# Queries and keys of an attention layer projected with features on partitions, instead of being transposed head by head

## The chip, the cores and the metric

The kernel runs on one core of a Trainium2 chip. The metric is the device time of one execution in microseconds. An execution computes a whole two-layer step of a small hybrid model on 128 context tokens and 1024 latent tokens.

## The reference

Only layer 0's attention matters here. From a normalised, modulated input h (1152 tokens x 1024) the reference projects queries, keys and values of two kinds of heads, rotates those of the second kind, and attends:

```python
nq, nk, nv, dq, dk, dv = split_cols(h @ w_in, ATTN_IN_SIZES)      # 512 columns each

def axial_rope(x):                       # differential heads, latent tokens only
    def rot(xh, p):                      # cos, sin of position p times 16 frequencies
        x1, x2 = xh[..., :quarter], xh[..., quarter:]
        return jnp.concatenate([x1 * cos - x2 * sin, x1 * sin + x2 * cos], axis=-1)
    return jnp.concatenate([rot(xf[..., :half], pos // GRID_W), rot(xf[..., half:], pos % GRID_W)], axis=-1)

def diff_attention(q, k, v, lam, lam_init):
    s = jnp.einsum('bqhcd,bkhcd->bhcqk', qb, k) * scale           # c: two maps a head
    p = jax.nn.softmax(s, axis=-1)
    p = p[:, :, 0] - lam * p[:, :, 1]
    o = jnp.einsum('bhqk,bkhe->bqhe', p, v)

def neighbourhood_attention(q, k, v, k_ctx, v_ctx, rpb):          # 8 x 16 window on a 16 x 64 grid, plus context
    s_win = jnp.einsum('brqhd,brikhd->bhrqik', qg, kg) * scale + bias
```

Keys and values of a 128-token cache are appended; context queries see context keys alone. The context's keys and values (not rotated) are outputs too.

## The kernel before

All is 32-bit. For a precise product each factor is split into a high half, rounded to the fast matmul type, and the low rest, and three matmuls are added (`mm3`). The normalised input is kept with features on partitions: eight tiles hH and hL of 128 features x 1152 tokens.

**Projection.** The columns of the heads are taken in eight groups: groups 0 to 3 are the four differential heads, 4 to 7 pairs of neighbourhood heads. A group has 384 columns: 128 of queries, of keys and of values. `attn_in` (L357) loads eight weight tiles wraw, splits each into wh and wl (L74, L75), and `proj_tok` (L332) computes nine tiles of 128 tokens x 384 columns with hH and hL as the stationary operands (L350 to L352). `sink` copies each tile from PSUM to ist (L368) and stores it to a table qkv in HBM (L369). A generator gives one step for the loads and one for each of the nine tiles.

**Preparing a head.** Scores need queries and keys with features on partitions. `prep_k` (L409) loads the head's keys token by token as kraw (L417, L418, L422), `stage` rotates them (L387 and L394 on VectorE, L397 on POOL), splits them (L405 on ScalarE, L406 on VectorE), and TensorE transposes them (L429) into K, copied by ScalarE (L434, L437). Ten tiles of tokens, two transposes each. `prep_q` (L440) does the same for one 128-token tile of queries: load qraw (L504, or L615 and L617), stage, four transposes (L446), one copy to Q (L448).

**Units and order.** A unit is a head and one of its nine query tiles. Its steps are a (queries), scores (L518, L519; L643 to L647 for neighbourhood heads), and weighted sums, which transpose the probabilities (L476) and multiply by the values (L482). `pipe` (L567) runs 36 units in a software pipeline: in each of 36 + 2 rounds seven slots, each followed by `fill`. `hook` prepares a new head's keys and values at its first unit. In the first stage the units are those of the differential heads, and `fill` pulls 0.28 of a step of the projections of groups 1 to 7 (gs) and 0.3 of a step of `ada_vec` a slot: 128x512 blocks aw of the modulation weights come from HBM (L128) and are accumulated on VectorE (L181). In the second stage the units are neighbourhood heads; bias tiles nab (L624), a mask nam (L587) and gathered values vw (L599, POOL's queue) come in, and `fill` pulls 0.34 of a step of the output projection: input rows xr (L699, L702) transposed to x (L705), attention outputs odr turned to mh and ml (`mix_k`), output weights owraw to owh and owl. Each transfer is on the queue of the engine that issues it; nearly all are on SP's.

The code gives instructions in this order, and a planner in the build, which models the engines' times, moves ready instructions ahead of waiting ones when it writes down each engine's final order. On the chip each engine and queue keeps that order.

## Time and profile before

| | us |
|---|---|
| median of 3 runs | 3835.94 (3829.51 to 3837.39) |
| the profiled execution | 3830.74 |
| its span in the trace | 3829.0 |
| TensorE busy | 3645.9 |
| VectorE busy | 2284.7 |
| ScalarE busy | 1399.5 |
| POOL busy | 1103.7 |

PE is TensorE, PEld its weight loads, DVE VectorE, ACT ScalarE, SP the engine that only issues transfers; SPq and ACTq are the queues of engines. A row of the trace names the line, the engine, the operation, the tile written and those read, how many, and times; "idle" is what the engine stood before such instructions, and behind the arrow what ended it. In rows of waits come the total in us, how many, and the longest. A matmul's busy time contains its latency, which overlaps with the next one's.

### The profile page before, as it was taken

How to read it: one execution, taken by the hardware profiler on the slowest of the kernel's cores; microseconds unless marked ns; L12 is line 12 of the kernel's file. 1: busy time of each engine (PE TensorE's matmuls, PEld its weight loads, DVE VectorE, ACT ScalarE, POOL GpSimd, SP SyncE). 2: the span in 40 equal slices, each digit the busy share in tenths (PEclk: the TensorE clock that was granted, in tenths of full speed). 3: DMA queues.
4: the chain of work that ended last, by engine and by line, in shares of the span. 5: the costliest groups of instructions: out<-in, count | busy, mean ns of one | idle time of the engine just before them, and what ended most of it. 6: DMA issues, size and time to landing. Idle time of an engine off the chain costs nothing.

```text
span 3829.0 us, 66995 instructions
## 1 busy us (share of the span) xinstructions
PE 3645.9 (95%) x24885; PEld 3428.2 (90%) x24885; DVE 2284.7 (60%) x5106; ACT 1399.5 (37%) x3361; POOL 1103.7 (29%) x1450
## 2 busy tenths in 40 slices
PE   7999997999999999999999998999998999999998
PEld 4899996999999999999989886877777899999998
DVE  6578874665855667765253655666666774444434
ACT  3444444555433333225232332233322533334222
POOL 2000002112323324333010323566652322333430
PEclk9999998999999999999999998999999999999999
DMA  6433325542133335433333345222223122223321
GB/s 209 124 91 100 115 77 127 140 106 60 58 99 104 101 101 160 153 113 99 96 122 117 120 135 199 64 75 74 77 65 101 55 62 77 73 74 108 114 89 62
DMA packets 425397, 392.14 MB, mean 102 GB/s; under 512 B 68172, under 2 KB 370376, under 8 KB 423536
## 3 DMA queue, kind: packets, MB, share of 16 engines
q1 hardware_dynamic: 406640, 376.29, 32.5%
q10 hardware_dynamic: 13152, 7.27, 0.7%
q0 software_dynamic: 5280, 4.31, 0.6%
q8 instruction: 197, 3.23, 0.4%
q14 instruction: 128, 1.05, 0.1%
HBM read 289.32 MB, written 98.33 MB: 101 GB/s over the span
## 4 chain that ended last, share of the span: by engine, by line
PE 73%; DVE 8%; DMA 7%; issue 4%; POOL 4%; ACT 2%; SPq 0%; DVEq 0%; ACTq 0%; POOLq 0%
PE mm L82 9%; PE mm L84 9%; PE mm L83 9%; PE A L1724 3%; PE A L1725 3%; PE A L1726 3%; PE o L482 2%; PE mm L350 2%; PE mm L352 2%; PE mm L351 2%; PE E L1724 2%; PE E L1725 2%; PE E L1726 2%; DMA aw<-in_w_ada_dram 2%; PE T L476 1%
## 5 line engine op out<-in xcount | busy, mean ns | idle before, releaser
L729 DVE SCALAR_TENSOR_TENSOR x<-mm,mod,x 128x128 f32<-128x128 f32 (+1 forms) x576 | 279.1, 512 | 263.1 <-PE mm L84 262.3
L1636 POOL TENSOR_TENSOR wl<-raw,wh 128x512 fp32r<-128x512 f32 x120 | 175.0, 1459 | 592.8 <-ACT wh L1635 582.6
L1635 ACT CAST wh<-raw 128x512 fp32r<-128x512 f32 x288 | 178.0, 619 | 294.8 <-PE A L1725 100.3
L181 DVE SCALAR_TENSOR_TENSOR aacc<-aw,v,aacc 128x512 f32<-128x512 f32 x280 | 235.4, 875 | 81.7 <-DMA aw<-in_w_ada_dram 81.7
L350 PE MATMUL mm<-wh,hH 128*128 128x384 f32 x576 | 201.1, 349 | 13.0 <-ACT wh L74 5.8
L352 PE MATMUL mm<-wh,hL 128*128 128x384 f32 x576 | 196.2, 342 | 4.6 <-DVE hL L261 4.6
L351 PE MATMUL mm<-wl,hH 128*128 128x384 f32 x576 | 197.7, 343 | 0.5 <-DVE wl L75 0.4
L82 PE MATMUL mm<-hH,wh 128*128 128x384 f32 x528 | 184.9, 351 | 2.6 <-ACT wh L74 2.6
L84 PE MATMUL mm<-hH,wl 128*128 128x384 f32 x528 | 180.9, 345 | 2.2 <-DVE rst L867 1.8
L83 PE MATMUL mm<-hL,wh 128*128 128x384 f32 x528 | 180.4, 342 | 0.0
L1636 DVE TENSOR_TENSOR wl<-raw,wh 128x512 fp32r<-128x512 f32 x168 | 121.6, 724 | 86.3 <-ACT wh L1635 84.8
L397 POOL TENSOR_TENSOR rm<-rm,rm 128x128 f32<-128x128 f32 (+1 forms) x40 | 27.1, 676 | 464.9 <-DVE rm L387 332.2
L75 DVE TENSOR_TENSOR wl<-wraw,wh 128x256 fp32r<-128x256 f32 (+1 forms) x184 | 88.8, 501 | 109.9 <-ACT wh L74 80.6
L1150 PE MATMUL A<-AR,BK 64*128 64x256 f32 x576 | 119.6, 423 | 31.8 <-DVE KK L1154 19.5
L524 ACT ACTIVATE P<-S,mx 128x384 f32<-128x384 f32 (+1 forms) x200 | 112.2, 570 | 86.3 <-DVE mx L522 84.1
L82 PE MATMUL mm<-mh,owh 128*128 128x384 f32 x384 | 139.4, 378 | 3.7 <-ACT mh L74 2.5
L83 PE MATMUL mm<-ml,owh 128*128 128x384 f32 x384 | 133.2, 347 | 0.0
L84 PE MATMUL mm<-mh,owl 128*128 128x384 f32 x384 | 131.8, 343 | 1.3 <-DVE owl L75 1.3
L350 PEld LDWEIGHTS mm<-wh,hH 128*128 128x128 f32 x576 | 110.4, 192 | 17.9 <-ACT ist L368 8.0
L1150 PEld LDWEIGHTS A<-AR,BK 64*128 64x128 f32 x576 | 77.5, 198 | 54.5 <-issue 18.4
L817 PE MATMUL mm<-wh,hH 128*128 128x256 f32 x432 | 124.0, 290 | 0.0
L818 PE MATMUL mm<-wl,hH 128*128 128x256 f32 x432 | 122.4, 285 | 0.0
(540 smaller groups left out, 12459.7 us busy)
## 6 DMA issues: line engine op xcount, KB each, us to landing
raw<-in_w_ffn_in_dram SPq DMA_DIRECT2D x176, 256.0 KB
aw<-in_w_ada_dram SPq DMA_DIRECT2D x160, 256.0 KB
raw<-hdr SPq DMA_DIRECT2D x132, 192.0 KB
hdr<-c SPq DMA_DIRECT2D x160, 144.0 KB
raw<-in_w_ffn_out_dram SPq DMA_DIRECT2D x88, 256.0 KB
F<-stg SPq DMA_DIRECT2D x34, 640.0 KB
stg<-st SPq DMA_DIRECT2D x12, 1536.0 KB
qkv<-ist SPq DMA_DIRECT2D x72, 192.0 KB
```

Of the source, the lines that this page charges most:

```text
L82: mm(out, lhsT=wh, rhs=xh, start=first, stop=False)
L83: mm(out, lhsT=wh, rhs=xl, start=False, stop=False)
L84: mm(out, lhsT=wl, rhs=xh, start=False, stop=last)
L181: nc.vector.scalar_tensor_tensor(acc[:, c, :], w[:, 0, :], s, acc[:, c, :], op0=ALU.mult, op1=ALU.add)
L350: mm(pt[:, :ncol], lhsT=hH[k][:, c], rhs=WH[k], start=k == 0, stop=False)
L351: mm(pt[:, :ncol], lhsT=hH[k][:, c], rhs=WL[k], start=False, stop=False)
L352: mm(pt[:, :ncol], lhsT=hL[k][:, c], rhs=WH[k], start=False, stop=k == KT - 1)
L729: self.nc.vector.scalar_tensor_tensor(x[f][:, c], pt[:, a:b], self.mod[l][jg][:, f, cd : cd + 1], x[f][:, c], op0=ALU.mult, op1=ALU.add)
L1150: mm(pts[h][:, j * 256 : j * 256 + 256], lhsT=BK[hs, j, :], rhs=AR[hs], start=True, stop=True)
L1636: eng.tensor_tensor(wl, w, wh, op=ALU.subtract)
L1724: mm(o, lhsT=wh[:, ks], rhs=xh, start=new and k == 0, stop=False, skip_group_check=True)
L1725: mm(o, lhsT=wh[:, ks], rhs=xl, start=False, stop=False, skip_group_check=True)
```

## The change

The projection computes queries and keys with the weights as the stationary operand, so that they come out with features on partitions, in three token groups of 384; the queries and keys of differential heads are rotated right behind it on those tiles (halves swapped by copies across partitions, one multiplication each with tables of sine and cosine that now have features on partitions, one addition). They are split there, and high and low half are stored to a table qf for each of queries and keys. The order of the features within a differential head is changed in the weights' split so that the swap moves 64 partitions at a time. Values are still needed with tokens on partitions: they are projected in the same way and transposed three at a time (`turn`), and stored to vt. Neighbourhood queries are put in the order of their windows when they are split and stored (`patches`, `store_hl`).

A head is prepared by a generator `heads_steps`: K and three tiles Q of 384 queries are loaded as they are, in transfers of 32 or 64 rows (of differential and neighbourhood heads; the stores have 128); only the cached keys are still staged and transposed. `heads_hook` starts it three units ahead of the head. The stepping of the projections becomes 0.53 of a step a slot, for 19 steps a group. Two of the four mix buffers are given elsewhere: three stay and one is opened for the last group.

```diff
...
-        for T in range(NT):
-            pt = self.t(self.nps, [P, 512], tag="mm")
-            c = slice(T * P, (T + 1) * P)
-            for k in range(KT):
-                mm = nc.tensor.matmul
-                mm(pt[:, :ncol], lhsT=hH[k][:, c], rhs=WH[k], start=k == 0, stop=False)
-                mm(pt[:, :ncol], lhsT=hH[k][:, c], rhs=WL[k], start=False, stop=False)
-                mm(pt[:, :ncol], lhsT=hL[k][:, c], rhs=WH[k], start=False, stop=k == KT - 1)
-            sink(T, pt)
...
+        if g < 4:
+            ok, ov = O[4][0, 0, :, j].rearrange("t c d -> t (c d)"), O[5][0, 0, :, j]
+        else:
+            ok, ov = (o[0, 0, :, 2 * j : 2 * j + 2].rearrange("t c d -> t (c d)") for o in (O[2], O[3]))
+        apart = lambda t: [t.rearrange("p (m r s d) -> p s m r d", r=4, s=2, d=16)[:, s] for s in range(2)] if g < 4 else [t]
+        dense = lambda t: [t.rearrange("p (m s r d) -> p s m r d", r=4, s=2, d=16)[:, s] for s in range(2)] if g < 4 else [t]
+        WH, WL = [], []
+        for k in range(KT):
+            raw = self.t(pool, [P, GW], tag="wraw")
+            src = w[k * P : (k + 1) * P, :].rearrange("p (m c) -> p m c", c=512)[:, blk : blk + 3, j * P : (j + 1) * P]
+            nc.sync.dma_start(raw.rearrange("p (m c) -> p m c", c=P), src)
+            wh = self.t(pool, [P, GW], F32R, tag="wh")
+            wl = self.t(pool, [P, GW], F32R, tag="wl")
+            for a in zip(dense(wh), dense(wl), apart(raw)):
+                self.split(*a)
+            WH.append(wh)
+            WL.append(wl)
+        yield
+        def turn(st, n):
+            pt = self.t(self.nps, [P, 512], tag="T")
+            for i in range(n):
+                nc.tensor.transpose(pt[:, i * P : (i + 1) * P], st[:, i * P : (i + 1) * P], self.ident)
+            o = self.t(pool, [P, GW], tag="ist")[:, : n * P]
+            for a in zip(apart(o), dense(pt[:, : n * P])):
+                nc.scalar.copy(*a)
+            return o
+        later = []
+        for m, scale in ((1, None if g < 4 else -0.125), (0, 0.125 if g < 4 else None), (2, None)):
+            ms = slice(m * P, (m + 1) * P)
+            for tg in range(TG):
+                for step in later:
+                    step()
+                later = []
+                sl = slice(tg * GW, (tg + 1) * GW)
+                pt = self.t(self.nps, [P, 512], tag="mm")
+                for k in range(KT):
+                    self.mm3(pt[:, :GW], WH[k][:, ms], WL[k][:, ms], hH[k][:, sl], hL[k][:, sl], k == 0, k == KT - 1)
+                if m == 2:
+                    st = self.t(pool, [P, GW], tag="ist")
+                    nc.scalar.copy(st, pt[:, :GW])
+                    yield
+                    o = turn(st, 3)
+                    dst = self.vt[g][sl, :]
+                    nc.sync.dma_start(dst.rearrange("(n p) c -> p n c", p=P), o.rearrange("p (n c) -> p n c", c=P))
+                    if tg == 0:
+                        nc.scalar.dma_start(ov, o[:, :P])
+                    yield
+                    continue
+                hl = self.t(pool, [P, 2, GW], F32R, tag="hl")
+                hi, lo = hl[:, 0, :], hl[:, 1, :]
+                x = pt[:, :GW]
+                if g < 4 or m == 1 and tg == 0:
+                    n = GW if g < 4 else P
+                    x = self.t(pool, [P, GW], tag="fx")
+                    nc.scalar.copy(x[:, :n], pt[:, :n])
+                    a = P if tg == 0 else 0
+                    sw = lo.bitcast(F32)
+                    for s in range(2):
+                        nc.scalar.copy(sw[64 * s : 64 * s + 64, a:], pt[64 - 64 * s : 128 - 64 * s, a:GW])
+                    ts = slice(tg * GW + a - P, (tg + 1) * GW - P)
+                    nc.vector.tensor_tensor(sw[:, a:], sw[:, a:], self.sin[:, ts], op=ALU.mult)
+                    nc.vector.tensor_tensor(x[:, a:], x[:, a:], self.cos[:, ts], op=ALU.mult)
+                    nc.vector.tensor_tensor(x[:, a:], x[:, a:], sw[:, a:], op=ALU.add)
+                    yield
+                if m == 1 and tg == 0:
+                    nc.sync.dma_start(ok, turn(x, 1))
+                if g >= 4:
+                    x = pt[:, :GW]
+                for u, v in self.patches(g, m, tg):
+                    nc.scalar.activation(v(hi), u(x), AF.Copy, scale=scale or 1.0)
+                if g >= 4:
+                    yield
+                def rest(g=g, m=m, tg=tg, x=x, hl=hl, scale=scale):
+                    hi, lo = hl[:, 0, :], hl[:, 1, :]
+                    for u, v in self.patches(g, m, tg):
+                        if scale is None:
+                            nc.vector.tensor_tensor(v(lo), u(x), v(hi), op=ALU.subtract)
+                        else:
+                            nc.vector.scalar_tensor_tensor(v(lo), u(x), scale, v(hi), op0=ALU.mult, op1=ALU.subtract)
+                    self.store_hl(g, m, tg, hl)
+                if g < 4:
+                    later.append(rest)
+                    rest()
+                yield
+    def patches(self, g, m, tg):
+        if g < 4 or m == 1:
+            same = lambda t: t
+            return [(same, same)]
+        n0 = P if tg == 0 else 0
+        out = [(lambda t: t[:, :n0],) * 2] if n0 else []
+        u = lambda t: t[:, n0:].rearrange("p (r w c) -> p r w c", w=4, c=16)
+        v = lambda t: t[:, n0:].rearrange("p (w r c) -> p r w c", w=4, c=16)
+        return out + [(u, v)]
+    def store_hl(self, g, m, tg, hl):
+        dst, a, hl = self.qf[g][m], tg * GW, hl.bitcast(F32)
+        if g < 4 or m == 1:
+            nc.sync.dma_start(dap(dst, a, [[TOK, P], [P * TOK, 2], [1, GW]]), hl)
+            return
+        r0, n0 = (0, P) if tg == 0 else (6 * tg - 2, 0)
+        nr = (GW - n0) // 64
+        for i in range(2):
+            if n0:
+                nc.sync.dma_start(dap(dst, i * P * TOK, [[TOK, P], [1, n0]]), hl[:, i, :n0])
+            sw = hl[:, i, n0:].rearrange("p (w r c) -> p w r c", w=4, c=16)
+            for rh in range(2):
+                a, b = max(r0, 8 * rh), min(r0 + nr, 8 * rh + 8)
+                if a < b:
+                    o = dap(dst, i * P * TOK + (1 + 4 * rh) * P + (a - 8 * rh) * 16, [[TOK, P], [P, 4], [1, (b - a) * 16]])
+                    nc.sync.dma_start(o, sw[:, :, a - r0 : b - r0, :].rearrange("p w r c -> p w (r c)"))
+    def heads_steps(self, g, cache, p, ps, head, values=None):
+        K = head["K"] = self.t(p, [P, 2, 10 * P], F32R, tag="K")
+        rows = lambda c: [(0, 32 * c, 32), (32, 64 + 32 * c, 32)] if g < 4 else [(0, 64 * c, 64)]
+        for c in range(2):
+            for i in range(2):
+                for o, r, n in rows(c):
+                    o += 64 * i
+                    nc.sync.dma_start(K[o : o + n, c, :TOK].bitcast(F32), dap(self.qf[g][1], (i * P + r) * TOK, [[TOK, n], [1, TOK]]))
+        raw = self.t(p, [P, P], tag="kraw")
+        nc.sync.dma_start(raw, cache)
+        yield
+        def queries(tg):
+            Q = head["Q", tg] = self.t(p, [P, 2, 2, GW], F32R, tag="Q")
+            for c in range(2):
+                for i in range(2):
+                    for o, r, n in rows(c):
+                        o += 64 * i
+                        src = dap(self.qf[g][0], r * TOK + tg * GW, [[TOK, n], [P * TOK, 2], [1, GW]])
+                        nc.sync.dma_start(Q[o : o + n, c, :, :].bitcast(F32), src)
+        queries(0)
+        yield
+        st = self.t(p, [P, 2, 2, 64], F32R, tag="st")
+        for c in range(2):
+            rv, sv = raw[:, 64 * c : 64 * c + 64], lambda i: st[:, c, i, :]
+            if g < 4:
+                rv = rv.rearrange("p (r s d) -> p s r d", s=2, d=16)
+                sv = lambda i: st[:, c, i, :].rearrange("p (s r d) -> p s r d", s=2, d=16)
+                nc.scalar.copy(sv(0), rv)
+                nc.vector.tensor_tensor(sv(1), rv, sv(0), op=ALU.subtract)
+                self.split(sv(0), sv(1), rv, -0.125)
+        yield
+            nc.tensor.transpose(pt[:, c * P : (c + 1) * P], st[:, c].rearrange("p b c -> p (b c)").bitcast(F32), self.ident)
+        nc.scalar.copy(K[:, :, 9 * P :], pt[:, : 2 * P].rearrange("p (c t) -> p c t", c=2))
+        yield
+        queries(1)
+        yield
+        if values is not None:
+            values()
+        yield
+        queries(2)
+        yield
+    def heads_upto(self, j, k, heads, gen):
+        if j not in heads:
+            heads[j] = {"n": 0}
+            heads[j]["gen"] = gen(j, heads[j])
+        while heads[j]["n"] < k:
+            heads[j]["n"] += 1
+            next(heads[j]["gen"], None)
+    def heads_hook(self, j, T, heads, gen):
+        self.heads_upto(j, 7 if T >= 2 else 6, heads, gen)
+        if T >= 6 and j < 7:
+            self.heads_upto(j + 1, (2, 4, 6)[T - 6], heads, gen)
...
+    def diff_prep(self, j, head, p, ps):
         nc, I = self.nc, self.I
-        src = self.qkv[j]
-        K = self.prep_k(j, I["cache_diff_k"][0, 0, :, j].rearrange("t c d -> t (c d)"), True, p, ps)
-        V = self.t(p, [P, 10, P], tag="V")
-        nc.sync.dma_start(V[:, 0:9, :], src[:, 2 * P :].rearrange("(n p) c -> p n c", p=P))
-        nc.sync.dma_start(V[:, 9, :], I["cache_diff_v"][0, 0, :, j])
-        ob = self.t(p, [P, NT, P], tag="ob")
-        ss = self.t(p, [P, NT], tag="oss", bufs=2)
-        return K, V, ob, ss
+        def values():
+            V = head["V"] = self.t(p, [P, 10, P], tag="V")
+            nc.sync.dma_start(V[:, 0:9, :], self.vt[j].rearrange("(n p) c -> p n c", p=P))
+            nc.sync.dma_start(V[:, 9, :], I["cache_diff_v"][0, 0, :, j])
+        return self.heads_steps(j, I["cache_diff_k"][0, 0, :, j].rearrange("t c d -> t (c d)"), p, ps, head, values)
...
-            raw = self.t(p, [P, 1, P], tag="qraw")
-            nc.sync.dma_start(raw[:, 0, :], self.qkv[j][T * P : (T + 1) * P, 0:P])
-            st["Q"] = self.prep_q(p, ps, raw, None if T == 0 else (self.cos[:, T - 1 : T, :], self.sin[:, T - 1 : T, :]))
+            if T == 0:
+                head[j]["ob"] = self.t(p, [P, NT, P], tag="ob"), self.t(p, [P, NT], tag="oss", bufs=2)
...
-            K, Q = head[j][0], st["Q"]
+            K, Q = head[j]["K"], head[j]["Q", T // 3][:, :, :, T % 3 * P : T % 3 * P + P]
...
+    def na_prep(self, j, head, p, ps):
+        hs = slice(2 * j, 2 * j + 2)
+        return self.heads_steps(4 + j, self.I["cache_na_k"][0, 0, :, hs].rearrange("t c d -> t (c d)"), p, ps, head)
...
-        mh = self.t(p, [P, TOK], F32R, tag="mh", bufs=4)
-        ml = self.t(p, [P, TOK], F32R, tag="ml", bufs=4)
+        mh = self.t(p, [P, TOK], F32R, tag="mh")
+        ml = self.t(p, [P, TOK], F32R, tag="ml")
...
-                self.wpool = _Bufs(wp, {"wraw": 3, "wh": 9, "wl": 9, "ist": 2, "aw": 2})
+                self.wpool = _Bufs(wp, {"wraw": 3, "wh": 9, "wl": 9, "ist": 2, "fx": 2, "hl": 2, "aw": 2})
...
-            return self.attn_in(g, hH, hL, wpool)
+            yield from self.first if g == 0 else self.attn_in(g, hH, hL, wpool)
+            done.add(g)
...
-        GS, AS, OS = 0.28, 0.3, 0.34
+        GS, AS, OS = 0.53, 0.3, 0.34
...
-        bp = _Bufs(both.enter_context(self.pool("kAB")), {"K": 2, "Q": 3, "pT": 2, "qraw": 2, "kraw": 2})
+        bp = _Bufs(both.enter_context(self.pool("kAB")), {"K": 2, "Q": 3, "pT": 2})
...
-            fin(self.first)
+            first = group(0)
+            for _ in range(12):
+                next(first)
+            self.heads_upto(0, 5, head, lambda j, h: self.diff_prep(j, h, dp, ps))
+            fin(first)
             self.nps = ps
             gs = itertools.chain.from_iterable(group(g) for g in range(1, 8))
+            def prep(j, h):
+                while j not in done:
+                    next(gs)
+                return self.diff_prep(j, h, dp, ps) if j < 4 else self.na_prep(j - 4, h, dp, ps)
             def hook(i):
-                j, T = divmod(i, NT)
-                if T == 0 and j < 4:
-                    head[j] = self.diff_prep(j, dp, ps)
+                if i < 4 * NT:
+                    self.heads_hook(*divmod(i, NT), head, prep)
...
-        op = _Bufs(self.oA, {"owraw": 1, "owh": 4, "owl": 4})
-        head = {}
+        op = _Bufs(self.oA, {"owraw": 1, "owh": 4, "owl": 4, "mh": 3, "ml": 3})
...
-                    head[j] = self.na_prep(j, dp, ps)
+                if i < 4 * NT:
+                    self.heads_hook(4 + i // NT, i % NT, head, lambda j, h: self.na_prep(j - 4, h, dp, ps))
...
-                    yield from self.mix_k(k, op, ps, ms)
+                    yield from self.mix_k(k, op if len(ms) < 3 else _Route(op, {"mh": more, "ml": more}, None), ps, ms)
...
+            more = es.enter_context(self.pool("oM"))
```

165 lines of the change are left out of this document (34 added, 131 removed).

## The prediction, made before the change was run

> **What bounds the kernel now.** I read the busy times first, then stretches of time cut at the borders of layer 0's stages, then what TensorE waited for in each, then its order of instructions.
>
> ```profile
> span 3829.0 us, 66995 instructions
> PE 3645.9 (95%) x24885; PEld 3428.2 (90%) x24885; DVE 2284.7 (60%) x5106; ACT 1399.5 (37%) x3361; POOL 1103.7 (29%) x1450
> ...
> core 0: us, PE busy (x) PEld busy (x) DVE busy (x) ACT busy (x) POOL busy (x), PEclk, DMA share, GB/s
> 61.00:130.00 69.00, 59.69 (x325) 57.20 (x325) 38.60 (x77) 20.61 (x44) 10.91 (x11) 0.93 0.43 123
> 130.00:604.00 474.00, 459.91 (x2980) 447.73 (x2979) 354.55 (x886) 223.94 (x722) 23.97 (x37) 0.99 0.32 96
> 604.00:670.00 66.00, 38.12 (x206) 33.70 (x205) 29.45 (x79) 27.37 (x74) 21.60 (x32) 0.74 0.67 159
> 670.00:893.00 223.00, 212.24 (x1602) 206.24 (x1601) 135.71 (x404) 122.81 (x315) 21.51 (x32) 0.98 0.45 116
> ```
>
> The change lies between 61 and 893 us. Four stretches: the projection of group 0 (start), differential attention with the other seven projections filled in (stage A), the crossing, and neighbourhood attention with the output projection filled in (stage B). TensorE is busy for 97% of A and 95% of B, VectorE for 75% and 61%: in A and B time is TensorE time. The crossing is different: 28 of its 66 us TensorE stands.
>
> ```profile
> PE mm L350 <- ACT wh L74: 5.2, 3, 3.4
> PE mm L350 <- ACT ist L368: 3.2, 6, 1.3
> ...
> PE T L476 <- DVE P L541: 9.2, 2, 7.7
> PE T L429 <- DVE st L406: 8.9, 4, 3.8
> PE S L643 <- DVE mx L649: 3.7, 4, 2.8
> PE T L705 <- DMA xr<-in_x_prompt_dram: 3.1, 1, 3.1
> ...
> PE T L446 <- ACT K L437: 2.3, 1, 2.3
> ```
>
> The first two rows are A's longest waits (us in total, times, longest): small. The others are from 600 to 900 us. Two of them, 8.9 and 2.3 us, are TensorE waiting for the staging of keys and queries that the change removes; the longest (9.2) is not.
>
> What a transpose costs cannot be had from its mean duration, since matmuls overlap. The order of TensorE's instructions (start, duration) gives it:
>
> ```profile
> 593.19 0.60 PE L476 MATMUL T<-ident,P 128*128 128x128 f32 x4
> 593.55 0.42 PE L350 MATMUL mm<-wh,hH 128*128 128x384 f32 x1
> 593.81 0.34 PE L351 MATMUL mm<-wl,hH 128*128 128x384 f32 x1
> 593.99 0.34 PE L352 MATMUL mm<-wh,hL 128*128 128x384 f32 x1
> ...
> L446 PE MATMUL T<-ident,st x288: 271/273/477, 127.9 to 870.9; 128*128 128x128 f32 x144
> L429 PE MATMUL T<-ident,st x160: 270/273/476, 108.5 to 832.4; 128*128 128x128 f32 x160
> ```
>
> Four transposes hold the array from 593.19 to 593.55, 0.36 us or 0.09 each. The wide matmul behind them takes 0.26 to the next start, where one among its like takes 0.18: each block costs 0.08 more. A block of four is 0.44 us, 0.11 a transpose. The 273 ns of the rows is latency. The rows also count what there is: 288 query transposes (4 for each of 72 units) and 160 of keys (20 a head).
>
> **The projection itself: no change.** 216 matmuls of 128x384 a group before; after, 3 column blocks x 3 token groups x 8 x 3 = 216 of the same width.
>
> **Transposes, the main term.** Removed: 288 + 160. Added for each of 8 groups: three blocks of three for the values, one for the context keys; for each head one block of two for the cached keys. With 0.09 a transpose and 0.08 a block:
> - Stage A and start: removed 36 blocks of four, 15.8 us, and 80 key transposes at 0.11, 8.8 us. Added 8 x (3 x 0.35 + 0.17) = 9.8 us and five cached blocks at 0.26, 1.3 us (head 4 is prepared in A now). Net 13.5 us less.
> - Stage B: removed 15.8 + 8.8, of which head 4's keys and first query, 2.6 us, stand in the crossing; added 3 x 0.26 = 0.8. Net 21 us less.
> TensorE runs without gaps in both, so I take A at 13 and B at 21. Bounds: if its work were wholly the limit, 35 together; if other engines took over at once, 0.
>
> **Key staging at a head's first unit.** It was emitted at the first unit; now loads start three units ahead. The 8.9 us waits on L429 are 5.3 in the crossing and 3.6 at 693 to 700 us. I take the 3.6 in B.
>
> **The crossing.**
>
> ```profile
> 607.03 1.04 ACT L74 CAST owh<-owraw 128x1024 fp32r<-128x1024 f32 x1 [3.87 <-DMA owraw<-in_w_out_attn_dram]
> 619.25 1.97 PE L476 MATMUL T<-ident,P 128*128 128x128 f32 x8 [7.66 <-DVE P L541]
> 635.51 1.97 PE L429 MATMUL T<-ident,st 128*128 128x128 f32 x8 [3.81 <-DVE st L406]
> 637.25 0.52 DVE L587 CAST nam<-sb 80x512 fp32r<-80x512 f32 x1 [1.72 <-DMA sb<-in_k_namask_dram]
> 655.96 0.30 PE L705 MATMUL T<-ident,xr 128*128 128x128 f32 x1 [3.10 <-DMA xr<-in_x_prompt_dram]
> ```
>
> Until 624 us ACT's in-order queue stands behind output weights that arrive late, and VectorE behind ACT; that stays. The keys of head 4 go out of 624 to 637, with 5.3 + 2.3 us of waits. But the mask tile is copied only at 637.25 and input rows still arrive late at 655.96: these are late next. Removing nothing that ends a wait gives 0; all 28 us idle would be the other bound. I take 6, nearest to the 7.6 of waits, less something for what stays. Other engines there: ten query loads and four key loads leave the crowded transfers too.
>
> **VectorE and ScalarE: covered, in A.**
>
> ```profile
> L387 DVE TENSOR_TENSOR rm<-qraw,cos x32: 281/292/295, 121.6 to 572.4; 128x128 f32<-128x128 f32 x32
> L387 DVE TENSOR_TENSOR rm<-kraw,cos x8: 682/692/693, 104.2 to 487.6; 128x512 f32<-128x512 f32 x8
> L406 DVE SCALAR_TENSOR_TENSOR st<-qraw,st x40: 272/282/295, 101.7 to 868.5; 128x128 fp32r<-128x128 f32 x40
> L448 DVE CAST Q<-T 128x512 fp32r<-128x512 f32 x35 | 24.1, 688 | 9.2 <-PE T L446 8.6
> L75 DVE TENSOR_TENSOR wl<-wraw,wh 128x384 fp32r<-128x384 f32 x47 | 26.5, 578 | 8.9 <-ACT wh L74 8.6
> L368 ACT COPY ist<-mm 128x384 f32<-128x384 f32 x60 | 28.9, 481 | 56.6 <-PE mm L352 52.6 <-issue 2.8 <-ACT wh L74 0.7
> ```
>
> VectorE, a differential head: before, keys 2 x 3 x 0.69 + 0.4, queries 8 x 2 x 0.29 + 9 x (0.28 + 0.69), weight splits 8 x 0.58: 22.6 us. After, rotation 6 x 3 x 0.56 (between 0.29 and 0.69), the low halves 6 x 0.56, and sixteen half-width splits at 0.36: 19.2 us. A neighbourhood group now takes its six low halves in A, some 3.9 us at 0.6. For all: -14 + 16 = +2 us on 354.55. ScalarE: a differential group gets 6 x 4 copies at 0.48 where it had nine copies, two dozen small casts and six key copies, about +3; a neighbourhood group +2; +20 us on 223.94 of 474. Both are hidden behind TensorE; if that cover went, the 20 us of ScalarE would count in part. POOL loses its additions, which nobody on the path waited for long: 0. In B, VectorE and ScalarE each lose about 40 us, also 0 by themselves.
>
> **Queues.** Transfers issued by SP between 61 and 893: stores 72 before; after, 10 a differential group (6 halves, 3 values, 1 keys) and 17 a neighbourhood group (3 + 10 + 3 + 1): 108. Head loads 15 a head before; 35 a differential head after (8 keys, 1 cache, 24 queries, 2 values), 19 a neighbourhood head: 120 becomes 216. ACT's queue loses eight output stores. So SP issues 132 more, at 0.32 to 0.59 us:
>
> ```profile
> L369 SPq DMA_DIRECT2D qkv<-ist x72: 319/322/503, 87.2 to 600.1; - x72
> L617 SPq DMA_DIRECT2D qraw<-qkv x32: 574/592/1761, 572.8 to 860.1; - x32
> SPq L369 <- ACT ist L368: 174.5, 53, 8.1
> SPq L128 <- DVE aacc L181: 39.7, 19, 9.7
> DVE aacc L181 <- DMA aw<-in_w_ada_dram: 7.6, 13, 1.0
> ```
>
> At 0.45 that is 59 us, spread over 830. SP already waits 174.5 us for stores' data, so it has room. Behind it are the modulation weights (aw), for which VectorE waits, in order, with everything queued behind: 7.6 us in A so far. A differential head's loads come in bursts of 17, 10 and 8 issues; the longest holds SP some 7.5 us, more than the 6.3 us between two aw loads (0.3 of a step a slot, seven slots in 474 / 36 = 13.2 us). Lower bound 0; upper, one such burst fully exposed at each of eight heads, 60 us. VectorE stands idle a quarter of A, so I take 4 us lost. POOL's queue keeps its 64 value gathers. Bytes: A moves 474 us x 96 GB/s = 45 MB; keys and queries are now stored as two halves and the queries read for both halves of the partitions, 1.2 MB more a group and 2.4 MB more a head, 20 MB in all. The share of 0.32 becomes about 0.46: hidden.
>
> **Weights at a group's start.** Steps are half as long (0.53 a slot for 19 steps, instead of 0.28 for 10), so from the last matmuls of a group to the first of the next there are 3 / 0.53 = 5.7 slots instead of 2 / 0.28 = 7.1: 2.7 us less to reload eight weight tiles, whose splits took 105.08 to 116.06 us at the first group. Bounds 0 and 7 x 2.7 = 19; the wait so far is 5.2, so I take 3 lost.
>
> **Start and end.** Keys come first and need all token groups early, but TensorE already waits for the low half of the input there, and head 0's staging runs behind group 1's matmuls: 0 (from +8 to -10). The last output group has three mix buffers and one opened late: 1 lost.
>
> **Sum:** -13 - 21 - 3.6 - 6 + 4 + 3 + 1 = -36 us. The profiled execution took 3830.74, so 3795; the median shown, 3835.94, is 5 above it, so 3800 for a median.
>
> **Rivals.**
> 1. *The crossing closes* (more gain). With queries ready, neighbourhood scores need only mask and bias; of the 28 us idle perhaps 18 go instead of 6, and bursts cost nothing (4): 3784 as median. Against: the mask at 637 and the late rows at 656.
>
> ```profile
> 630.00:640.00 10.00, 4.67 (x20) 3.78 (x21) 4.95 (x16) 2.74 (x6) 4.75 (x8) 0.50 0.97 183
> 640.00:650.00 10.00, 7.82 (x34) 7.28 (x34) 3.74 (x15) 4.64 (x16) 4.26 (x7) 0.50 0.84 204
> ```
>
> The granted clock is 0.50 in these 20 us, behind the gaps, and the 12.5 us of work in them would take 6 at full clock: a shorter gap saves up to 6 more, 3778. The Trainium skill, "TensorE: Matmul & The Clock Gate", "What's actually happening", states this as a rule: half clock after an idle window of about 3.4 us, full clock again after a busy one. The two rows agree with it; no run here shows yet whether the gap falls short enough.
> 2. *Another engine takes over* (no change): with TensorE lighter, VectorE's chains (28.9 us it waited on ScalarE's exponentials in A) set the pace; A, B and the crossing give only 10, and 8 are lost: about 3834. For it: 75% with bursts; against: TensorE's small waits.
> 3. *SP becomes the bound* (slower): stores wait for VectorE's low halves, loads for stores, aw stands behind both, VectorE behind aw. At the full 60 us instead of 4: -40 + 60 = +20, 3856. It decides once more than two thirds of the bursts are exposed. Against: 132 issues are 59 us of an idle queue. The Trainium skill, "DMA: Bandwidth & Descriptors", "Anatomy of one DMA", says that a wait sits on the issuing sequencer, not on the DMA engines; the 174.5 us row agrees.
> 4. *The change doesn't do what it says*: transposes were taken into gaps and their removal opens gaps: as 2.
>
> **How the numbers follow.** Forecast (gain of 10 to 50) 0.60; crossing closes, 0.18; no change, 0.09; slower, 0.13. 0.2% is about 7.7 us, what a measurement can tell from no change here: faster 0.78, same 0.09, slower 0.13. The forecast's own range is 3786 to 3826. For 8 in 10 I reach down to 3768 (crossing and the clock, with spread) and up to 3834, the no-change case; beyond are the slow case and a tail of the first.
>
> **What would show it.** Transposes by keys and queries fall from 448 to 96 with the values' included; A is 8 to 16 us shorter, B 18 to 26; no wait for staging at the first unit of a head. Wrong if VectorE's wait for aw grows past 20 us, if the first matmul of a group waits for wh more than 15 us in all, or if TensorE's busy share in A falls below 94%.

## The result: slower by 1.15%

The changed kernel takes 3879.47 us (median of 4, 3874.71 to 3882.32) against 3836.24 (median of 4, 3829.51 to 3837.39): ratio 1.0115, 95% interval 1.0098 to 1.0133. The profiled execution took 3877.96, 47 us more than the one before. The page's span and busy times of the kernel after:

```profile
span 3876.2 us, 66185 instructions
...
PE 3656.6 (94%) x24533; PEld 3436.9 (89%) x24533; DVE 2240.5 (58%) x5030; ACT 1392.4 (36%) x3329; POOL 1068.0 (28%) x1410
```

TensorE issues 352 instructions less and is busy longer. The stretches of layer 0 after, cut where the stages now lie (columns as before: TensorE, its weight loads, VectorE, ScalarE, POOL, granted clock, DMA share, GB/s):

```profile
61.00:130.00 69.00, 54.55 (x278) 50.02 (x276) 47.69 (x111) 28.15 (x76) 9.10 (x8) 0.88 0.50 147
130.00:618.00 488.00, 461.29 (x2882) 445.33 (x2881) 338.55 (x846) 235.90 (x747) 0.00 (x0) 0.97 0.46 131
618.00:687.00 69.00, 44.10 (x214) 40.25 (x213) 23.87 (x72) 23.18 (x62) 21.10 (x32) 0.65 0.81 177
687.00:911.00 224.00, 200.35 (x1381) 195.46 (x1381) 105.02 (x332) 98.82 (x230) 21.92 (x33) 0.90 0.62 144
```

In A the share (0.46) and TensorE's part (94.5%) are as forecast, but A is 14 us longer (488 against 474) where 13 less were forecast. In B TensorE's 212 us busy at clock 0.98 became 200 at 0.90, the transfers' share went from 0.45 to 0.62, and the stretch is as long as before (224 against 223). Below, the stages are cut at the first and last starts of their scores instead, which is the same cut in every kernel; by it 1 us is lost up to the first neighbourhood score (645.4 and 646.6 us) and 15 in B (234.8 and 249.4).

**Where the 47 us lie.** The first FFN matmul starts at 1012.3 us before and 1034.3 after: 22 us are lost in attention. The recurrent scan's first matmul starts at 2341.6 and 2366.2, its last starts at 2899.6 and 2948.7: 24.5 us more are lost in the scan, whose code the diff does not touch. The stretches between and behind agree within 3 us. In the profiles the scan's stretch reads, before, after, and in the kernel with one added memset (e5, below):

```profile
2341.00:2900.00 559.00, 516.55 (x4040) 426.50 (x4040) 373.33 (x869) 172.26 (x409) 321.98 (x735) 0.95 0.30 86
```
```profile
2366.00:2949.00 583.00, 536.51 (x4038) 446.84 (x4040) 365.21 (x869) 173.92 (x407) 322.88 (x735) 0.91 0.29 82
```
```profile
2362.00:2920.00 558.00, 518.51 (x4036) 427.13 (x4036) 368.86 (x869) 172.21 (x408) 321.60 (x735) 0.95 0.30 86
```

The same number of instructions, but in another written order: 706 of TensorE's 1160 scan instructions (runs of one kind counted once) stand elsewhere than before; in e5, 10 do. In the changed kernel's order single waits are longer and the clock is lower (after first, then e5):

```profile
PE A L1217 <- DVE KK L1221: 23.6, 13, 3.7
```
```profile
PE A L1217 <- DVE KK L1221: 19.6, 17, 1.5
```

The order is not all of it. In e16 (below) TensorE's instructions of the scan stand exactly as in e5, and yet its profiled execution, the slowest of twelve, spent 575 us there, at a lower clock:

```profile
2350.00:2925.00 575.00, 542.11 (x4038) 449.40 (x4036) 374.56 (x867) 171.93 (x407) 319.91 (x733) 0.91 0.28 83
```

So single profiles of one order differ by 17 us, and by 24 in e6 and e9 (experiment 3), as much as the loss. That 20 us hang on the later order is read from medians: 3879 with the changed kernel's order and 3855 in e5, and no execution of either lies in the other's range. By what the order acts is not shown.

**The transposes did go.** Those of queries, keys and values are now 72 + 8 + 16 = 96, where 448 stood:

```profile
L361 PE MATMUL T<-ident,ist x72: 270/273/422, 111.5 to 620.7; 128*128 128x128 f32 x72
...
L361 PE MATMUL T<-ident,fx x8: 271/300/477, 92.6 to 559.2; 128*128 128x128 f32 x8
```
```profile
L499 PE MATMUL T<-ident,st x16: 270/273/282, 111.1 to 838.5; 128*128 128x128 f32 x16
```

To see what that was worth I took the time from each TensorE record's start to the next one's start, and put what lies behind an instruction's end aside as a gap. For the two kernels with a barrier behind attention (e1, e2: nearly the same later order), 3427 and 3287 records between 50 and 640 us, 1866 and 1659 from 640 us to the first norm:

| records, us | start, A, crossing: before | after | B and the last group: before | after |
|---|---|---|---|---|
| all transposes | 550, 60.1 | 403, 45.5 | 598, 67.8 | 393, 49.4 |
| matmuls of the projections | 1728, 316.9 | 1728, 320.9 | 408, 75.9 | 408, 78.3 |
| scores of 128x384 | 384, 75.0 | 384, 78.4 | 128, 28.1 | 128, 27.6 |
| bias selection, short scores, weighted sums | | | 732, 88.8 | 730, 100.3 |
| gaps | 45.3 | 49.7 | 16.7 | 42.8 |

Transposes give 14.6 and 18.4 us, close to the 13.5 and 21 forecast. In B the gaps take back 26 and the wider spacing of the other matmuls 13.

What the gaps from 640 us to the first norm wait for after the change (e2, TensorE's longest, then VectorE's waits for transfers):

```profile
PE S L710 <- DVE mx L716: 18.0, 5, 10.2
PE T L549 <- ACT pT L551: 8.2, 3, 7.4
PE o L555 <- DVE ost L735: 6.8, 7, 2.0
PE T L772 <- DMA xr<-in_x_prompt_dram: 3.6, 1, 3.6
PE T L828 <- DMA xr<-odr: 3.4, 2, 2.5
```
```profile
DVE sb L716 <- DMA nab<-rpbd: 27.1, 8, 9.5
DVE ost L735 <- DMA odr<-ost: 8.1, 2, 5.2
```

Most of it is transfers, or VectorE that waits for transfers: the bias tiles nab first (27.1 us; 4.6 in e1), then stored outputs and input rows. The busy tenths of the 16 DMA engines from 640 to 900 us, 6.5 us a digit, before and after, show the difference:

```profile
DMA  8996566762459953222224986752200034352003
...
DMA packets 42954, 31.88 MB, mean 123 GB/s; under 512 B 5298, under 2 KB 41758, under 8 KB 42928
```
```profile
DMA  6788989677987999887716915898965351222251
...
DMA packets 40715, 40.29 MB, mean 155 GB/s; under 512 B 6510, under 2 KB 38102, under 8 KB 40694
```

Before, full stretches alternate with stretches of 2 and 3; after, they are full for most of 200 us. The megabytes grew by a quarter, the number of packets did not. An average of 0.45 was no free half. Where a transfer is late (here stored outputs), TensorE stands and then runs slowly:

```profile
810.00:820.00 10.00, 6.67 (x28) 6.48 (x28) 2.32 (x11) 2.82 (x7) 5.18 (x9) 0.50 0.90 163
820.00:830.00 10.00, 9.99 (x44) 9.90 (x44) 3.07 (x10) 2.94 (x6) 2.66 (x4) 0.50 1.01 169
850.00:860.00 10.00, 10.00 (x74) 10.00 (x73) 5.54 (x15) 2.67 (x8) 0.00 (x0) 1.00 0.23 62
```

The second and third are stretches without gaps: at half clock TensorE got through 44 instructions, at full clock through 74. The clock rule that the prediction cites from the Trainium skill ("TensorE: Matmul & The Clock Gate", "What's actually happening") is half clock after an idle window of about 3.4 us and full clock after a busy one. The rows agree with half clock behind gaps, but not with the lengths: the longest of the gaps in the first row is 2.4 us, and the second row is 10 us without a gap at half clock.

### The profile page after: what moved, and what is told of

The parts are those of the page before. It is cut to its first block, busy times and chain, and to the rows that moved or that the text cites. A ratio compares the mean times of both kernels' runs of the same rounds, so it can differ in the third digit from the quotient of the medians.

```text
span 3876.2 us, 66185 instructions
## 1 busy us (share of the span) xinstructions
PE 3656.6 (94%) x24533; PEld 3436.9 (89%) x24533; DVE 2240.5 (58%) x5030; ACT 1392.4 (36%) x3329; POOL 1068.0 (28%) x1410
## 4 chain that ended last, share of the span: by engine, by line
PE 62%; DMA 7%; DVE 5%; POOL 4%; issue 2%; ACT 1%; SPq 0%; ACTq 0%; DVEq 0%; POOLq 0%
PE mm L82 9%; PE mm L84 9%; PE mm L83 8%; PE A L1791 3%; PE A L1792 3%; PE A L1793 3%; PE E L1791 2%; PE E L1792 2%; PE E L1793 2%; DMA F<-stg 2%; POOL MB L1268 1%; PE o L555 1%; PE A L1217 1%; PE mm L884 1%; POOL tf L1267 1%
## 5 line engine op out<-in xcount | busy, mean ns | idle before, releaser
L796 DVE SCALAR_TENSOR_TENSOR x<-mm,mod,x 128x128 f32<-128x128 f32 (+1 forms) x576 | 278.7, 512 | 257.5 <-PE mm L84 256.8
L82 PE MATMUL mm<-hH,wh 128*128 128x384 f32 x1104 | 389.0, 353 | 23.2 <-ACT wh L74 11.1
L83 PE MATMUL mm<-hL,wh 128*128 128x384 f32 x1104 | 380.0, 344 | 9.4 <-DVE hL L261 9.4
L84 PE MATMUL mm<-hH,wl 128*128 128x384 f32 x1104 | 380.4, 346 | 3.0 <-DVE rst L934 2.4
L82 PEld LDWEIGHTS mm<-hH,wh 128*128 128x128 f32 x1104 | 212.4, 193 | 38.9 <-ACT wh L74 13.4
L670 POOL DMA_DIRECT2D vw<-vt x64 | 43.0, 677 | 696.8 <-DVE nab L653 569.0
L83 PEld LDWEIGHTS mm<-hL,wh 128*128 128x128 f32 x1104 | 213.1, 193 | 12.5 <-DVE hL L261 9.7
L84 PEld LDWEIGHTS mm<-hH,wl 128*128 128x128 f32 x1104 | 212.5, 193 | 8.1 <-issue 2.9
L75 DVE TENSOR_TENSOR wl<-wraw,wh 128x256 fp32r<-128x256 f32 (+2 forms) x216 | 91.3, 447 | 112.3 <-ACT wh L74 83.1
L886 PE MATMUL mm<-wh,hL 128*128 128x256 f32 x432 | 122.0, 283 | 0.0
```

The costliest lines, as they stand in the source:

```text
L82: mm(out, lhsT=wh, rhs=xh, start=first, stop=False)
L83: mm(out, lhsT=wh, rhs=xl, start=False, stop=False)
L84: mm(out, lhsT=wl, rhs=xh, start=False, stop=last)
L796: self.nc.vector.scalar_tensor_tensor(x[f][:, c], pt[:, a:b], self.mod[l][jg][:, f, cd : cd + 1], x[f][:, c], op0=ALU.mult, op1=ALU.add)
```

## The experiments

Single executions of one kernel spread over 20 to 30 us here, and A's last score over some 8, so medians are compared as differences to the kernel before of the same call, whose medians were 3831 to 3836. Most kernels carry a barrier or an unread memset behind attention, only to give the scan the order it had before, or nearly.

**1. Splitting attention from what follows.** e1 and e2 are before and after with

```diff
             xp, x, np_, hp, hH, hL = self.attn(hp, hH, hL, wes)
+            tc.strict_bb_all_engine_barrier()
```

> The kernel before, with one barrier of all engines behind layer 0's attention, so that the planner starts the rest from the same point in every kernel that has it. Both theories: the barrier costs the overlap of the last norm with the first feed-forward matmuls, 0 to 8 us over the kernel before; the scan (2342 to 2900 us in the trace of before, 559 us from the first to the end of its matmuls on L1150 and L1296) stays within 5 us of that.

> The changed kernel with the same barrier. In it the planner gives the scan nearly the order of the kernel before (29 of 1156 of its TensorE instructions stand elsewhere, against 706 in the changed kernel). Theory: of the 43 us lost about 22 are in the attention and 24 in the scan, lost to the planner's other order alone; then this kernel is 18 to 28 us above the one before with the barrier, and its scan takes 559 us within 6. Rival: the scan is slower for another reason (clock, place of its data in memory); then it is 40 to 48 us above, and the scan takes about 583 us.

e1: 3829.45, 5 below the kernel before (ratio 0.999, 0.9977 to 1.0004). e2: 3860.44, 26 above (1.006, 1.0043 to 1.0076). So attention alone loses, and the rest of the loss goes with the later order. e5 shows the latter without a barrier, by a memset that nothing reads:

```diff
+            with self.pool('pad') as pp:
+                nc.vector.memset(self.t(pp, [P, 64], tag='pad'), 0.0)
```

> The changed kernel, without a barrier, with one more instruction: VectorE clears a 128x64 tile that nobody reads, between layer 0's attention and its feed-forward. With it the planner writes the scan in the order of the kernel before but for 10 of 1160 TensorE instructions. Theory, the scan's loss of some 24 us is the planner's order alone: 3853 to 3865, and a scan of 558 us within 5 (first L1150-matmul to last L1296-matmul of the kernel before). Rival, another reason: 3875 to 3884, and a scan of 583.

3854.97, 23 above (1.006, 1.0037 to 1.0083): 20 us of the 43 come back, and the scan takes 558 us again in its profile.

**2. Is it the queue or the shape of the transfers?** e3 issues the loads of K and Q from ScalarE's queue; e7 changes how many rows a transfer has (loads of keys 128, of queries 64, stores 32 or 64).

```diff
-                    nc.sync.dma_start(K[o : o + n, c, :TOK]...
+                    nc.scalar.dma_start(K[o : o + n, c, :TOK]...
```

> As the changed kernel with the barrier, but keys and queries of the heads are loaded from ScalarE's queue instead of SP's; the order behind the barrier is that of the kernel before with the barrier. Theory A, SP's order: small transfers (bias, input rows, modulation weights) stand behind the heads' loads on SP; then 8 to 20 us less than the changed kernel with the barrier. Theory B, the 16 transfer engines themselves are full in these bursts, whichever queue issues: within 5 us of it. If ScalarE's time for issuing (some 150 of 0.4 us) counts: up to 15 us more.

> The changed kernel with the barrier; keys (and the differential heads' queries) are stored so that a head's keys come back in two transfers of 128 rows instead of eight of 32 or four of 64, and the differential queries in four of 64 instead of eight of 32; the stores are of 32 or 64 rows instead. The same bytes, with the clear instruction. Theory shape: 10 to 25 us less than the changed kernel with the barrier. Theory bytes: within 6 of it. If short stores hurt as much as short loads: up to 8 more.

e3: 3873.17, 39 above (1.0091, 1.0062 to 1.0121). e7: 3863.83, 32 above (1.0083, 1.0059 to 1.0108). Neither is better than e2. In e7's profile B takes 250.1 us, as in e2 (250.3), so rows don't matter there. In e3's it takes 257.0: another queue gains nothing, though ScalarE's time for issuing could hide a gain of SP's, which these runs don't separate.

**3. Are bytes hidden?** First from the changed kernel: e4 loads the keys twice, e6 leaves the low query half away for one half of the partitions.

```diff
+                    for _ in range(2):
                         nc.sync.dma_start(K[o : o + n, c, :TOK]...
```
```diff
-                nc.tensor.matmul(S[:, :ch], lhsT=Q[:, c, 1, :], rhs=kk, start=False, stop=True)
+                nc.tensor.matmul(S[:, :ch], lhsT=Q[:64, c, 1, :], rhs=kk[:64], start=False, stop=True)
```

> As the changed kernel with the barrier, but every head's keys are loaded twice (1.2 MB more a head, the same result); behind the barrier the order is that of the kernel before with the barrier. If the heads' loads are what costs the attention its time: 8 to 25 us more than the changed kernel with the barrier, most of it in the neighbourhood stage, where the transfers' share is 0.9 already. If the loss lies in PSUM, weights or the order of the projections: within 4 us.

> The changed kernel with the barrier; the low half of a query is loaded for one half of the partitions only, and its product runs over 64 rows (it leaves out the product of the two low halves). A quarter of the queries' bytes fewer: 0.59 MB a head, 4.7 MB in all, with as many transfers. The same clear instruction keeps the planner's order of the rest. Theory bytes: doubling the keys cost 22 us for 9.4 MB, so 9 to 14 us less than the changed kernel with the barrier (3860.4). Theory shape (transfers of 32 and 64 rows are what is slow, whatever their bytes): 0 to 6 less. Theory PSUM and weights: within 3.

e4: 3882.38, 48 above (1.012, 1.0102 to 1.0138), 22 more than e2. That fits bytes, but 13 of the 22 lie before A's end, where the first scores start 6 us later and TensorE once waits 4.4 us for queries loaded behind the doubled keys, so it is not bytes alone. e6: 3943.38, 111 above (1.028, 1.0252 to 1.0307), far outside every theory; its matmuls tell why (last section). It says nothing on bytes.

Then on the kernel before. e9 and e10 add 96 transfers that nothing waits for, spread or in bursts.

```diff
+                if i < 4 * NT and i % NT == 6:
+                    for n in range(12):
+                        self.extra()
```

> The kernel before, with a barrier and an unread memset behind layer 0's attention (they keep the later order), and 96 added transfers of 128 rows x 1536 B (192 KB each, weights to an unread table in HBM), twelve a head, four in three units, 18.9 MB in all in stages A and B. Nothing reads them. If bytes cost what the doubled keys cost in the changed kernel (2.3 to 3 us a MB), 43 to 57 us above the barrier kernel before (3829): 3872 to 3886. If they are hidden, as the prediction costed them, up to 5: 3829 to 3835. If only bursts cost, this one, which is spread, stays below 3845.

> The same 96 transfers, but the twelve of each head all issued at its seventh unit, as the changed kernel issues the next head's loads from there on. Bytes alone: as the spread kernel, within 8 us. If it is the burst (a transfer that TensorE needs stands behind them in the queue): 15 us or more above the spread one. Hidden: 3829 to 3835.

3860.88 and 3861.78, both 30 above (1.0069, 1.0045 to 1.0094; 1.0089, 1.0061 to 1.0117). Both missed their mark: transfers that depend on nothing were moved to the start by the planner, as e9's first two stretches show:

```profile
61.00:130.00 69.00, 50.45 (x249) 42.12 (x248) 36.97 (x67) 15.94 (x34) 15.60 (x11) 0.91 0.92 285
130.00:618.00 488.00, 469.95 (x3035) 457.31 (x3034) 357.62 (x891) 227.35 (x732) 27.60 (x39) 0.99 0.33 98
```

In attention the loss came before the first differential score (128 us became 152); A still moved 98 GB/s, and B took 235.6 and 235.8 us against 234.4 in e1. The rest of it, in the profiles, is the scan: 580 and 571 us, where e6 with the same order took 555. So e13 adds transfers that read what the stage itself has just stored:

```diff
             nc.sync.dma_start(self.qkv[g][T * P : (T + 1) * P, :], st)
+            if g and T:
+                self.extra(self.qkv[g][T * P - P : T * P, :])
...
+                if j < 4 and T >= 3:
+                    for n in range(2):
+                        self.extra(dap(self.odr[j - 1 if j else 7], (2 * T + n) % 3 * P * GW, [[GW, P], [1, GW]]))
```

> The kernel before with the barrier and an unread memset, and added transfers that cannot be moved to the start, since each reads what the stage itself has just stored: in A eight copies of 192 KB a group (the projected tiles, 11.0 MB), in B twelve of 192 KB a head (outputs of the head before, 9.4 MB), to an unread table in HBM. Bytes theory (1.6 to 3 us a MB): 33 to 60 above the barrier kernel before (3829): 3862 to 3890, with the first norm 20 or more later and TensorE's waits in B ended by bias tiles and input rows. If bytes by themselves are hidden and the changed kernel's loss is in when its loads are issued and what waits for them: at most 10 above: 3829 to 3840.

3861.37, 27 above (1.0067, 1.0042 to 1.0092). And it says where: A, with 11 MB more, ended at 605.9 us against 609.4 in e1. B, with 9.4 MB more, took 255.7 instead of 234.4.

Last, the changed kernel with loads taken out of one stage: in e17 neighbourhood heads 5 to 7 use head 4's keys and queries, in e18 differential heads 1 to 3 use head 0's. The results are other ones; the scores' matmuls stay. The edit of e17:

```diff
     def na_prep(self, j, head, p, ps):
+        if j > 0:
+            head.update(self.head4)
+            return iter(())
+        self.head4 = head
```

> The changed kernel with the barrier and unread memsets for the scan's order, in which neighbourhood heads 5 to 7 use the keys and queries of head 4 instead of loading their own: it leaves out 10.6 MB of loads in stage B (and the staging of three heads' cached keys), the matmuls stay. If bytes in B cost 2.1 us a MB (e13), 22 below the barrier kernel after (3860): 3835 to 3841, B some 228 instead of 250 us. If the loads are the whole loss of B, the predicted B (210) comes back: 3815 to 3825. If they are not what B loses time to: 3855 or more.

> The same for stage A: differential heads 1 to 3 use the keys and queries of head 0, 10.6 MB of loads left out there, values are loaded as before. If bytes in A are hidden (e13's A, with 11 MB more, was not longer): the last differential score within 4 of 620 us, and 3855 to 3862 in all. If bytes count in A as they do in B: 15 to 22 us earlier, 3838 to 3845.

e17: 3833.24, 1 above (0.9991, 0.9971 to 1.0011): 26 us come back, near the 24 that e13's 2.3 us a MB give for 10.6 MB. e18: 3859.14, 27 above (1.0073, 1.0046 to 1.0099), as e2. Loads count in B and are hidden in A. B in one stretch, from the first to the last neighbourhood score, in e1 (before), e13 (before, more bytes), e2 (after) and e17 (after, fewer bytes):

```profile
642.00:876.00 234.00, 219.44 (x1609) 213.43 (x1609) 140.13 (x414) 126.81 (x329) 32.12 (x48) 0.96 0.49 128
```
```profile
640.00:896.00 256.00, 229.31 (x1613) 221.63 (x1612) 139.58 (x415) 128.25 (x330) 32.17 (x48) 0.92 0.57 156
```
```profile
642.00:892.00 250.00, 209.99 (x1379) 204.75 (x1379) 111.77 (x349) 101.47 (x237) 43.03 (x64) 0.85 0.68 156
```
```profile
642.00:866.00 224.00, 195.51 (x1371) 190.81 (x1372) 110.97 (x354) 98.20 (x235) 43.01 (x64) 0.92 0.54 135
```

The second and third column from the right are clock and share. Length times GB/s gives 30, 40, 39 and 30 MB: the length follows the bytes, in either kernel. The two with 40 MB both move 156 GB/s, and at 30 MB the changed kernel's B is 12.6 us shorter by the scores' first and last starts (221.8 against 234.4). Three kernels of the last part (e11, e12, e16) load queries for half the partitions and lie between: 35 MB, and 238.6, 240.3 and 240.6 us, as in e11:

```profile
650.00:888.00 238.00, 204.22 (x1374) 199.77 (x1374) 110.53 (x343) 100.51 (x235) 57.46 (x82) 0.88 0.63 147
```

The nine profiles of the changed kernel with 38 to 39 MB in B lie between 245.5 (e8) and 257.0 (e3), so a step of 10 MB is clear of their spread.

**4. Bursts, or bias tiles that stand behind them?** e14 loads the bias tiles a unit earlier, e15 the heads in eleven pieces.

```diff
+                if i + 1 < 4 * NT:
+                    units[i + 1][0].load()
```
```diff
-        self.heads_upto(j, 7 if T >= 2 else 6, heads, gen)
-        if T >= 6 and j < 7:
-            self.heads_upto(j + 1, (2, 4, 6)[T - 6], heads, gen)
+        self.heads_upto(j, 11 if T < 2 else T + 10, heads, gen)
+        if T >= (6 if j == 0 else 2) and j < 7:
+            self.heads_upto(j + 1, T - 1 if T < 7 else T, heads, gen)
```

> The changed kernel with the barrier, bias tiles of neighbourhood heads loaded one unit (6.5 us) earlier, into six buffers instead of four; same bytes. If TensorE's gaps in B (42 us after, 17 before) are bias tiles that come late behind head loads: the gaps fall to some 25 and the half clock behind them too, 20 to 30 below the barrier kernel after (3860): 3830 to 3840. If the transfers as a whole are the limit, another one is late instead (input rows, attention outputs): 3855 to 3862. The scan's order is the slower one by some instructions here (156 of 1156 moved), which may cost up to 5.

> The changed kernel with the barrier, the loads of a head in eleven pieces over ten units, from the second unit of the head before, instead of in bursts of 17, 10 and 8 from its seventh; same bytes, same issues. If what counts is that a transfer stands behind a burst: 10 to 20 below the barrier kernel after: 3840 to 3850. If bytes count and not their place: 3856 to 3862.

e14: 3876.34, 42 above (1.0098, 1.0065 to 1.0131); its gaps from 640 to 940 us were 51 us, not 25. e15: 3862.39, 28 above (1.0069, 1.0046 to 1.0093). At equal bytes neither an earlier issue of the bias tiles nor smaller bursts gave anything back; B took 256.8 and 248.9 us.

**5. Versions.** e8 copies neighbourhood groups' projections out of PSUM before they are split; e11 loads queries for 64 partitions and lets POOL copy them to the others; e12 does both; e16 adds e14 and e15.

```diff
-                if g < 4 or m == 1 and tg == 0:
-                    n = GW if g < 4 else P
-                    x = self.t(pool, [P, GW], tag="fx")
-                    nc.scalar.copy(x[:, :n], pt[:, :n])
+                x = self.t(pool, [P, GW], tag="fx")
+                nc.scalar.copy(x, pt[:, :GW])
...
-                for i in range(2):
+                for i in range(1):
...
+                nc.gpsimd.tensor_copy(Q[64:P, c, :, :], Q[:64, c, :, :].bitcast(F32))
```

> The changed kernel with the barrier; the neighbourhood groups' queries and keys too are copied out of PSUM first, so that the bank of the next projection is free before the low halves are made; with the clear instruction. In the changed kernel TensorE waited 8.4 us for these low halves. Theory PSUM: 6 to 15 us less than the changed kernel with the barrier, all of it before the last differential scores. Theory bytes or shape: within 5, since waits move on to the next late thing.

> The changed kernel with the barrier, queries loaded for partitions 0 to 63 alone and copied to 64 to 127 by POOL (48 copies of 64x768), memset behind attention: 9.4 MB less to move, 96 fewer head loads, the same matmuls. Bytes theory (2.3 to 3 us a MB): 22 to 28 below the barrier kernel after (3860): 3832 to 3838. If the doubled keys cost by their lateness at a head's start and not by bytes, or the loss sits in the matmuls' order: 3855 to 3862. If the copies come late or disturb VectorE: above 3865.

> The changed kernel without a barrier, the copied half of the queries, neighbourhood groups copied out of PSUM first, and two unread memsets behind attention so that the scan has the order it had before. Bytes theory: the copied half's gain (22 to 28) and 5 of the PSUM copies from the padded kernel after (3855): 3822 to 3828, below the kernel before by 2 to 10. If bytes don't matter: 3848 to 3855.

> The changed kernel without a barrier and with all that should help: queries copied for the upper partitions (9.4 MB less), neighbourhood groups copied out of PSUM first, loads spread, bias tiles a unit early, one unread memset behind attention for the scan's order. The kernel with copy and PSUM alone took 3838 (before 3831). If lateness of the bias and bursts matter: 3815 to 3828, faster than before. If not: 3834 to 3840.

| | median | above before | ratio |
|---|---|---|---|
| e8 | 3855.26 | 23 | 1.006 (1.0042 to 1.0077) |
| e11 | 3855.16 | 24 | 1.0061 (1.0043 to 1.0079) |
| e12 | 3837.89 | 7 | 1.0014 (0.9999 to 1.0029) |
| e16 | 3838.61 | 4 | 1.0006 (0.9987 to 1.0026) |

None beats the kernel before; the last two cannot be told from it. One thing in their traces is steady. The last differential score is at 610.6, 609.2 and 608.0 us in the three that copy out of PSUM, and between 618.1 and 628.4 in e2, e5, e11, e14, e15, e17 and e18, which don't: e2's row, then e8's.

```profile
L589 PE MATMUL S<-K,Q x200: 219/339/688, 118.2 to 620.1; 128*128 128x384 f32 x95, 128*128 128x128 f32 x5
```
```profile
L585 PE MATMUL S<-K,Q x200: 222/339/686, 117.1 to 610.6; 128*128 128x384 f32 x95, 128*128 128x128 f32 x5
```

So about 10 us of A went to PSUM tiles that the split held. Why e8 and e11 gain 2 or 3 us each in the median and both together 19 (some 3 of them by the barrier left out, e5 against e2) stays open in part: in the profiles e11's B is 11.7 us shorter than e2's, but starts 7.7 later, and e8 is 13.6 ahead of e2 at B's last score and 7.5 at the end. Single executions differ by more than that.

## Why the prediction was wrong

Forecast 3800 in a range of 3768 to 3834; it came out at 3879, outside the range, on the side given 0.13, and by another way than rival 3.

- **"Bytes: ... hidden" is the step that failed.** The count was right (A's share 0.46, as forecast), and so was the word "hidden" for A: e13 and e18 changed A's bytes by 11 MB in either direction and its end moved by 3.5 and 2 us. But the sum weighed the bytes in A alone. B's heads load three times what they did, and B had no room: 9.4 MB more cost the kernel before 21 us of B (e13), and 10.6 MB less gave the changed one 28.5 us of B back, 26 in the median (e17). The mean share of 0.45 in B had no term; the slices behind it (8996566762459953...) show engines that ran full in bursts, while A's, here from 350 to 610 us before at the same 6.5 us a digit, reach 7 at most there:

```profile
DMA  4422157464311001366442211255150110002033
```

- **B, -25 forecast, +16 measured.** The transposes gave 18 of 21 us. Of the difference of 41, loads are 26 to 29 (e17). The other 12 to 15 stay open: with e17's bytes B gains 12.6 and not 25, and bias tiles still come late in it, as VectorE's waits in e1 and e17 show:

```profile
DVE sb L649 <- DMA nab<-rpbd: 4.6, 3, 2.1
```
```profile
DVE sb L720 <- DMA nab<-rpbd: 20.0, 9, 5.3
```

- **A -13, crossing -6, queue +4, weights +3: together -12 forecast, 0 measured** (first neighbourhood score 641.8 in e1, 642.0 in e2). Transposes gave 14.6 us, as sized. A missed term is PSUM: the low halves of neighbourhood groups are computed from the PSUM tile itself, and the next matmuls wait until VectorE has let go of it (A's longest waits after):

```profile
PE mm L82 <- ACT wh L74: 7.5, 5, 3.7
PE mm L82 <- DVE hl L421: 4.2, 2, 2.5
PE mm L82 <- DVE hl L419: 4.2, 3, 3.4
```

  That was costed with VectorE's "+2 us", as hidden; with the tiles copied out (e8) the first neighbourhood score comes at 633.2, 8.6 before e1 and near the 12 forecast. All of that is in the crossing (32.4 us in e1, 21.9 in e2, 22.6 in e8), which shrank by more than 6 and by less than rival 1 had it; why A itself gives nothing even then stays open.
- **The last output group**, +1 forecast: from the last neighbourhood score to the first norm 41.4 us in e1, 46.8 in e2. Not tested further.
- **The scan** was in no term. Some 20 us of the median go with an order that a planner writes for the whole program, and that an edit 1300 us earlier, or one unread memset (e5), turns over. Why one order takes 558 us in one execution and 575 in another (e5, e16) stays open.
- **Rival 3** (SP): loads on another queue gain nothing (e3), and VectorE's wait for modulation weights grew from 7.6 us only to this:

```profile
DVE aacc L181 <- DMA aw<-in_w_ada_dram: 16.8, 18, 1.8
```

- **What would show it wrong.** None of the three signs set for "wrong" came: 16.8 us of waits against 20, 7.5 for weights against 15, TensorE busy for 94.5% of A against 94. All three watched A. No sign was set for B's transfers, where most of attention's loss was. Of the signs for it the 96 transposes came, and no wait for staging; A and B did not get shorter.

## What to carry to other kernels

Cost added bytes stage by stage, against the slices of the DMA share and not its mean: a stage whose slices already touch 0.9 pays for each MB (here 2 to 3 us) even at a mean of 0.45. When work is taken from the bounding engine, the stage's transfers must fit into the shorter time as well. And where a build plans the order of the whole program, compare the written order and the granted clock of untouched stages over several executions before looking for a cause in the edit.

## What the hardware showed unexpectedly

e6 alternates matmuls of 128 and of 64 rows. TensorE's order in it (start, duration):

```profile
400.22 0.34 PE L590 MATMUL S<-K,Q 128*128 128x384 f32 x1
400.48 0.44 PE L591 MATMUL S<-K,Q 64*128 64x384 f32 x1
400.85 0.45 PE L590 MATMUL S<-K,Q 128*128 128x384 f32 x1
401.23 0.44 PE L591 MATMUL S<-K,Q 64*128 64x384 f32 x1
401.60 0.44 PE L590 MATMUL S<-K,Q 128*128 128x384 f32 x1
```

From start to start 0.37 us, where two matmuls of 128 rows one behind the other take 0.17 to 0.18: half the contraction costs twice the time here, 0.2 us more at each change of size. In all of attention the products of queries and keys took 236 us from start to next start, against 125 in e2; the gaps fell from 92 to 52 us, and the kernel's median came out 83 us above e2's. The Trainium skill, "TensorEngine Tiling (Array Packing)", "Key Properties", states that a change of tiling mode drains the array. The rows show what a change costs, not the drain itself.
